# SSD output transposed one projection later, first convolutions ahead of the dt chain, and gates dealt anew, in a hybrid encoder layer

## Chip, cores and metric

One core of a Trainium2 chip runs the whole layer in one program. The metric is the device time of that program in microseconds (us), the median of several runs. Engines: PE (TensorE, matmuls), DVE (VectorE), ACT (ScalarE), POOL (GpSimd), SP (SyncE, which only issues transfers here).

## What is computed

A sequence of 1024 tokens of width 1024 goes through one encoder layer, in fp32. The reference, cut to what matters here:

```python
h = rmsnorm(x, norm_mix)
proj = h @ w_in            # q, k, v | z | x, B, C | dt | gate_a, gate_b
attn = windowed_gqa_sink(q, k, v, attn_sink)       # 16 heads, 4 kv heads, |t-s| <= 128
ssd = ssd_branch(z, xbc, dt_raw, ...)              # 8 groups of 4 heads
merged = sigmoid(gate_a) * (attn @ w_attn_branch) + sigmoid(gate_b) * (ssd @ w_ssd_branch)
x = x + merged @ w_out
x = x + cross_attention(rmsnorm(x, norm_cross), rmsnorm(mem, norm_mem), w_xq, w_xkv, w_xo)
x = x + square(relu(rmsnorm(x, norm_ffn) @ w_up)) @ w_down
return rmsnorm(x, norm_final)

def ssd_branch(z, xbc, dt_raw, ...):
    xs, B, C = split(silu(depthwise_conv_5(xbc) + conv_b))
    dt = softplus(dt_raw + dt_bias)                # 32 heads, two directions
    y = scan_forward(xs, dt, B, C) + scan_backward(xs, dt, B, C) + d_skip * xs
    y = grouped_rmsnorm(y * silu(z)) * norm_g
```

Both scans go in 8 chunks of 128 tokens: within a chunk y is (C B^T times a decay matrix) times x, and between chunks a state is carried on.

## The kernel before

Every fp32 matmul is made of three matmuls on a high and a low part of its operands (`mm3`, L78 to L86): one of 128x512 outputs per k, 8 k's and two halves make one projection of 128 channels by 1024 tokens, 48 matmuls, which land in one PSUM tile of two banks (pool pg, two buffers). Smaller PSUM tiles (pool pp, four buffers of one bank) hold the states, steps and transposes. Weights come as raw tiles of 128x1024 through SP's queue; ACT makes the high part (`whi`, L66), POOL the low part (`wlo`, L67).

Start: after the norm, `dt_part` (L210 to L290) projects dt and works out softplus, running sums (two scans, L270 and L271) and exponentials on DVE and ACT, the dt chain; its results are transposed on PE (`dtt`, L289).

SSD phase: for each of 8 groups a list of jobs (L535 to L571) gives PE's order by hand: four convolution projections (`conv_job`: two x tiles, B, C), one gate projection (`gate_job`), and z (`z_job`). A job yields after each chunk of three matmuls, and a table hangs other work on the chunk's number: while group g is projected, group g-1 is scanned. `conv_post` (L340 to L358) takes a convolution from PSUM: one ACT operation (L345) and four taps on DVE (L349, L351) that read PSUM and so hold its tile, then tanh on ACT (L353) and a closing DVE operation (L354). `state` (L443) makes chunk states, `back` (L460) runs the backward recursion on POOL, `prep` (L467) makes the decay matrix ef of the next chunk: two loads of rows on ACT's queue, two selects on POOL, eight exponentials on ACT (L484, L485), a sum (L486) and a product (L487) on DVE. `step` (L489) calls `prep` for the chunk below and does one chunk: matmuls with ef (L499) and with the state (yo, L503), then t from yo (L507, which frees the PSUM tile of yo), the D skip on POOL (L511, L513), sums and gate (L515 to L517), squares (L518), and after every fourth chunk the norm's scale on four yz tiles (L522). `yt` (L525) transposes four yz tiles into two PSUM tiles (L530), which ACT takes (`yts`, L532, one buffer) and SP writes to memory.

Only PE's order is fixed by hand in this phase; the Tile scheduler orders the other engines' queues.

Attention (`attn_phase`, L574) goes over 4 kv heads and 8 blocks of queries: scores (sps, L657), softmax, transposes (pt, L680), values (op, L689 and L690). Its blocks are woven with gate projections (`gate_block`, L705), which the table `ATT_GATES` assigns to kv heads, and with the next kv head's projections. The merge (`merge_cross_phase`, L709) begins with the gates of `END_GATES` (L727); beside them it loads the attention's and the SSD's outputs (at, yk: SP's queue, then a copy on ACT, L723, and a difference on DVE, L724), 8 and 16 tiles of 256 KB and three weights, into a pool that opens when the attention's pool is released. Its matmuls (mps) read those tiles in order, three for each of 24 tiles.

Of the kernel before, what the change touches and what calls it, by code (L numbers as in the profile page):

```python
# [29 lines left out]
ATT_GATES = ((11,), (12,), (13,), ())  # L30
# [67 lines left out]
def wsplit(w, nk=NK):  # L98
    hi = w[0].rearrange("p (k c) -> p k c", k=nk)
    lo = w[1].rearrange("p (k c) -> p k c", k=nk)  # L100
    return [(hi[:, k], lo[:, k]) for k in range(nk)]
# [108 lines left out]
def dt_part(kx, ins, dr, p0):  # L210
# [99 lines left out]

def ssd_phase(kx, ins, dr):
# [4 lines left out]
    with tc.tile_pool(name="p1", bufs=1) as sp, tc.manual_schedule(engines={mybir.EngineType.PE}):  # L316
# [7 lines left out]
        class Group:  # L324
            pass

        gs = []
        for g in range(NG):
            q = Group()
            q.g, q.hs, q.cx = g, slice(4 * g, 4 * g + 4), []  # L330
            gs.append(q)

        def fm_chunks(ps, w, halves=(0, 1)):
            ws = wsplit(w)
            for h in halves:
                for k in range(NK):
                    mm3(kx, ps[:, h * 512:(h + 1) * 512], ws[k], act_pair(kx.hT[h], k), k == 0, k == NK - 1)
                    yield

        def conv_post(q, i, ps):  # L340
            tag = ("cx", "cx", "cB", "cC")[i]
            j = 4 * q.g + i
            cw = lambda k: kx.cw[:, 5 * j + k:5 * j + k + 1]
            acc = ca.tile([P, S], F32, tag=tag, bufs=2 if i < 2 else 1, name=tag)
            A.activation(acc, ps, AF.Identity, bias=kx.cb[:, j:j + 1], scale=cw(2))  # L345
            for k in (1, 3, 0, 4):
                o = k - 2
                if o < 0:
                    V.scalar_tensor_tensor(acc[:, -o:], ps[:, :S + o], cw(k), acc[:, -o:], ALU.mult, ALU.add)  # L349
                else:  # L350
                    V.scalar_tensor_tensor(acc[:, :S - o], ps[:, o:], cw(k), acc[:, :S - o], ALU.mult, ALU.add)  # L351
            th = ca.tile([P, S], F32, tag="tab", bufs=2, name="th")
            A.activation(th, acc, AF.Tanh)  # L353
            V.scalar_tensor_tensor(acc, th, 1.0, acc, ALU.add, ALU.mult)  # L354
            if i < 2:
                q.cx.append(acc)
            else:
                setattr(q, ("BT", "CT")[i - 2], acc)  # L358

        def psum_g(name):  # L360
            return kx.pg.tile([P, S], F32, tag="g", name=name)

        def conv_job(q, i):
            def load():
                return wload(kx, ins["wssd"][q.g, i])

            def run(w):
                ps = psum_g("cps")
                yield from fm_chunks(ps, w)
                conv_post(q, i, ps)  # L370
            return load, run

        def first_job(q):
            def load():
                return [wload(kx, ins["wssd"][q.g, i]) for i in range(2)]

            def run(ws):
                pss = [psum_g("cps") for _ in range(2)]
                for h in range(2):
                    for i in range(2):  # L380
                        yield from fm_chunks(pss[i], ws[i], (h,))
                for i in range(2):
                    conv_post(q, i, pss[i])
            return load, run

        def gate_job(m):
            def load():
                return wload(kx, ins["wg"][m])

            def run(w):  # L390
                ps = psum_g("gps")
                yield from fm_chunks(ps, w)
                gt = ca.tile([P, 2, 512], F32, tag="tab", bufs=2, name="gt")
                for h in range(2):
                    A.activation(gt[:, h], ps[:, h * 512:(h + 1) * 512], AF.Tanh, scale=0.5)
                    nc.sync.dma_start(dr.gt[m][h], gt[:, h])
            return load, run
# [69 lines left out]
        def prep(q, c):  # L467
# [12 lines left out]
            q.ef = ef = sp.tile([P, 4, P], F32, tag="ef", bufs=3, name="ef")  # L480
# [8 lines left out]
        def step(q, c):  # L489
# [24 lines left out]
            y = q.yz[j] = sp.tile([P, 256], F32, tag="yz", bufs=6, name="yz")  # L514
# [25 lines left out]
        for g in range(NG):  # L540
            q, o = gs[g], gs[g - 1]
            scan = lambda *cs: [(step, o, c) for c in cs] if g else []
            if g == 0:
                job(first_job(q), {})
                job(gate_job(0), {})
                job(conv_job(q, 2), {})
                job(conv_job(q, 3), {8: [(tm_x, q)]})
            else:
                job(conv_job(q, 0), {8: [(step, o, 7)], 16: [(step, o, 6)]})
                job(conv_job(q, 1), {8: [(step, o, 5)], 16: [(step, o, 4)]})  # L550
                job(gate_job(g), {8: [(step, o, 3)], 16: [(step, o, 2), (yt, o)]})
                job(conv_job(q, 2), {8: [(step, o, 1)], 16: [(step, o, 0)]})
# [6 lines left out]
        job(gate_job(8), {5: [(step, q, 7)], 10: [(step, q, 6)], 16: [(step, q, 5)]})  # L559
        job(gate_job(9), {5: [(step, q, 4)], 10: [(step, q, 3)], 16: [(step, q, 2), (yt, q)]})  # L560
        job(gate_job(10), {5: [(step, q, 1)], 10: [(step, q, 0)]})
# [519 lines left out]
```

## Time and profile before

| what | value |
|---|---|
| median of 3 runs | 2541.56 us (2540.14 to 2542.85) |
| the profiled execution | 2542.49 us |
| its span, first to last instruction | 2540.7 us |
| mean granted clock of PE | 0.986 |
| busy: PE, PE's weight loads | 96%, 80% |
| busy: DVE, ACT, POOL | 49%, 40%, 37% |
| moved by DMA | 212 MB, 84 GB/s |

The times in views of the trace count from the first instruction of the profiled execution. The granted clock is a share of full speed (2.4 GHz); its other level is half of it (1.2 GHz), so that a stretch with a value between the two had some of both. A wait is idle time of an engine that ended when another one released it. Busy times are averages over stages with different limits; what an edit is worth is read at its place.

### The profile page before, as it was taken

What the parts mean: (1) busy time and instruction counts of PE and PEld (TensorE: products, weight loads), DVE (VectorE), ACT (ScalarE), POOL (GpSimd) and SP (SyncE); (2) the same over time, 40 slices, a digit from 0 to 9 for tenths busy, and PEclk for the clock granted to TensorE, in tenths of its full rate; (3) what the DMA queues carried; (4) which work ended last, traced back from release to release, by engine and by line L of the source; (5) the groups of instructions that cost most, each with busy time, mean ns of one, the idle gap of its engine ahead of it and who ended that gap; (6) DMA issues with size and microseconds to landing.
All of it is one profiled execution on the core that took longest, in us unless ns stands there. A gap on an engine that the chain in (4) does not pass through costs nothing.

```text
span 2540.7 us, 32190 instructions
## 1 busy us (share of the span) xinstructions
PE 2446.7 (96%) x12348; PEld 2035.1 (80%) x12348; DVE 1241.4 (49%) x2033; ACT 1024.6 (40%) x2114; POOL 934.5 (37%) x808
## 2 busy tenths in 40 slices
PE   7899999999999999999989999999999999999998
PEld 6687887878778788877768878888988888888887
DVE  5656555565655553465554252335543434343435
ACT  5436445463644544576664242235432121212112
POOL 4334526354452643354444444224332131312120
PEclk9899999999999999999999999999999999999999
DMA  6313223132322312111115363411121010101101
GB/s 221 100 50 117 67 84 111 56 116 64 103 75 76 116 66 76 48 40 55 51 37 204 133 224 128 171 50 67 59 75 67 34 67 34 66 35 58 42 34 67
DMA packets 135913, 212.20 MB, mean 84 GB/s; under 512 B 9680, under 2 KB 84560, under 8 KB 135760
## 3 DMA queue, kind: packets, MB, share of 16 engines
q1 hardware_dynamic: 65152, 171.86, 19.6%
q10 hardware_dynamic: 70608, 38.28, 5.3%
q8 instruction: 97, 1.59, 0.3%
q14 instruction: 56, 0.46, 0.1%
HBM read 183.63 MB, written 26.48 MB: 83 GB/s over the span
## 4 chain that ended last, share of the span: by engine, by line
PE 74%; POOL 7%; DVE 6%; ACT 5%; DMA 4%; issue 3%; POOLq 0%; SPq 0%; ACTq 0%; DVEq 0%
PE ups L81 5%; PE ups L86 5%; PE ups L85 5%; PE dps L86 4%; PE dps L81 4%; PE dps L85 4%; PE mps L85 3%; PE mps L86 3%; PE mps L81 3%; DMA rows<-d_cs 3%; PE zp L86 2%; PE zp L85 2%; PE zp L81 2%; PE cps L81 2%; PE cps L85 2%
## 5 line engine op out<-in xcount | busy, mean ns | idle before, releaser
L67 POOL TENSOR_TENSOR wlo<-raw,whi 128x1024 fp32r<-128x1024 f32 x170 | 412.4, 2427 | 458.8 <-ACT whi L66 441.7
L66 ACT ACTIVATE whi<-raw 128x1024 fp32r<-128x1024 f32 x172 | 181.6, 1056 | 356.8 <-PE mps L85 117.4
L962 DVE TENSOR_TENSOR x<-x,dps 128x512 f32<-128x512 f32 x256 | 175.8, 688 | 124.6 <-PE dps L86 123.0
L67 POOL TENSOR_TENSOR wdl<-raw,wdh 128x1024 fp32r<-128x1024 f32 x32 | 76.0, 2396 | 423.2 <-ACT wdh L66 423.2
L81 PE MATMUL cps<-kt,whi 128*128 128x512 f32 x512 | 217.0, 424 | 0.0
L86 PE MATMUL cps<-kt,wlo 128*128 128x512 f32 x512 | 202.6, 396 | 0.0
L85 PE MATMUL cps<-kt,whi 128*128 128x512 f32 x512 | 202.5, 395 | 0.0
L81 PE MATMUL ups<-kt,whi 128*128 128x512 f32 x512 | 199.7, 390 | 0.0
L85 PE MATMUL ups<-kt,whi 128*128 128x512 f32 x512 | 199.4, 390 | 0.0
L86 PE MATMUL ups<-kt,wlo 128*128 128x512 f32 x512 | 199.2, 389 | 0.0
L81 PE MATMUL dps<-wdh,u 128*128 128x512 f32 x512 | 199.2, 389 | 0.0
L85 PE MATMUL dps<-wdl,u 128*128 128x512 f32 x512 | 199.2, 389 | 0.0
L86 PE MATMUL dps<-wdh,u 128*128 128x512 f32 x512 | 199.2, 389 | 0.0
L936 DVE TENSOR_TENSOR u<-ups,ru 128x512 f32<-128x512 f32 x64 | 44.2, 690 | 256.4 <-ACT ru L934 254.6
L66 ACT ACTIVATE wdh<-raw 128x1024 fp32r<-128x1024 f32 x32 | 32.3, 1053 | 229.9 <-PE dps L86 229.7
L81 PE MATMUL gps<-kt,whi 128*128 128x512 f32 x256 | 109.7, 429 | 12.6 <-DVE cx L351 12.6
L85 PEld LDWEIGHTS cps<-kt,whi 128*128 128x128 f32 x512 | 98.6, 193 | 24.2 <-issue 5.0
L81 PEld LDWEIGHTS cps<-kt,whi 128*128 128x128 f32 x512 | 98.6, 193 | 24.0 <-issue 5.0
L86 PEld LDWEIGHTS cps<-kt,wlo 128*128 128x128 f32 x512 | 98.1, 192 | 21.7
L464 POOL TENSOR_TENSOR cb_t<-prev,dec 128x256 f32<-128x256 f32 x48 | 32.2, 672 | 224.8 <-ACT prev L458 222.2
L81 PEld LDWEIGHTS ups<-kt,whi 128*128 128x128 f32 x512 | 96.1, 188 | 20.4 <-ACT kt L143 0.3
L85 PEld LDWEIGHTS ups<-kt,whi 128*128 128x128 f32 x512 | 96.1, 188 | 20.0 <-DVE kt L144 0.2
(312 smaller groups left out, 6482.8 us busy)
## 6 DMA issues: line engine op xcount, KB each, us to landing
rows<-d_cs ACTq DMA_DIRECT2D x128, 256.0 KB, 4.2
raw<-in_wssd_dram SPq DMA_DIRECT2D x48, 512.0 KB, 3.8
raw<-in_wsb_dram SPq DMA_DIRECT2D x32, 512.0 KB, 3.2
raw<-in_wup_dram SPq DMA_DIRECT2D x32, 512.0 KB, 3.2
raw<-in_wdn_dram SPq DMA_DIRECT2D x32, 512.0 KB, 3.2
x<-in_x_dram SPq DMA_DIRECT2D x16, 512.0 KB, 7.2
raw<-in_wg_dram SPq DMA_DIRECT2D x16, 512.0 KB, 4.2
d_y<-yts SPq DMA_DIRECT2D x32, 256.0 KB, 2.8
```

The lines of the kernel that those rows point to most:

```text
L66: nc.scalar.activation(hi, raw, AF.Copy)
L67: (eng or nc.gpsimd).tensor_tensor(lo, raw, hi.bitcast(F32), ALU.subtract)
L81: i = mm(out, l[0], r[0], start=first, stop=False)
L85: mm(out, l[0], r[1], start=False, stop=False)
L86: mm(out, l[1], r[0], start=False, stop=last)
L464: G.tensor_tensor(heads(t), heads(prev[:, c, 1]), decay(q, 1, c), ALU.mult)
L936: V.tensor_tensor(u2, pv, r, ALU.mult)
L962: V.tensor_tensor(xh, xh, ps, ALU.add)
```

## The change

Four edits, of order and buffers alone:

- The first `yt` of a group moves from chunk 16 of the gate job, right behind step 2, to chunk 16 of the next convolution job, ahead of step 0. For this yz has 8 buffers instead of 6, and ef 2 instead of 3.
- The first two convolutions of group 0 are issued in `dt_part`, ahead of the dt chain (`first_tiles`); group 0's gate moves behind the convolutions of B and C.
- The last group's steps hang on the gates 8 and 9 alone, every four chunks, instead of on 8, 9 and 10.
- Gates 10 to 13 are dealt to the four kv heads; the last kv head had none. Gates 14 and 15 stay in the merge's code.

```diff
-ATT_GATES = ((11,), (12,), (13,), ())
+ATT_GATES = ((10,), (11,), (12,), (13,))
 END_GATES = (14, 15)
...
             A.activation(e[o:o + 32], ps[64 + 32 * d:96 + 32 * d, h * N:(h + 1) * N], AF.Copy)
+    first_tiles(kx, ins)
     V.tensor_tensor(u, u, e, ALU.add)
...
+def first_tiles(kx, ins):
+
+    q = kx.first = Group(0)
+    ws = [wload(kx, ins["wssd"][0, i]) for i in range(2)]
+    pss = [psum_g(kx, "cps") for _ in range(2)]
+    for h in range(2):
+        for i in range(2):
+            for _ in fm_chunks(kx, pss[i], ws[i], (h,)):
+                pass
+    for i in range(2):
+        conv_post(kx, q, i, pss[i])
...
-            q.ef = ef = sp.tile([P, 4, P], F32, tag="ef", bufs=3, name="ef")
+            q.ef = ef = sp.tile([P, 4, P], F32, tag="ef", bufs=2, name="ef")
...
-            y = q.yz[j] = sp.tile([P, 256], F32, tag="yz", bufs=6, name="yz")
+            y = q.yz[j] = sp.tile([P, 256], F32, tag="yz", bufs=8, name="yz")
...
             if g == 0:
-                job(first_job(q), {})
-                job(gate_job(0), {})
                 job(conv_job(q, 2), {})
-                job(conv_job(q, 3), {8: [(tm_x, q)]})
+                job(conv_job(q, 3), {})
+                job(gate_job(0), {8: [(tm_x, q)]})
             else:
                 job(conv_job(q, 0), {8: [(step, o, 7)], 16: [(step, o, 6)]})
                 job(conv_job(q, 1), {8: [(step, o, 5)], 16: [(step, o, 4)]})
-                job(gate_job(g), {8: [(step, o, 3)], 16: [(step, o, 2), (yt, o)]})
-                job(conv_job(q, 2), {8: [(step, o, 1)], 16: [(step, o, 0)]})
+                job(gate_job(g), {8: [(step, o, 3)], 16: [(step, o, 2)]})
+                job(conv_job(q, 2), {8: [(step, o, 1)], 16: [(yt, o), (step, o, 0)]})
                 job(conv_job(q, 3), {8: [(tm_x, q)], 16: [(yt, o)]})
...
         q = gs[7]
-        job(gate_job(8), {5: [(step, q, 7)], 10: [(step, q, 6)], 16: [(step, q, 5)]})
-        job(gate_job(9), {5: [(step, q, 4)], 10: [(step, q, 3)], 16: [(step, q, 2), (yt, q)]})
-        job(gate_job(10), {5: [(step, q, 1)], 10: [(step, q, 0)]})
+        job(gate_job(8), {4: [(step, q, 7)], 8: [(step, q, 6)], 12: [(step, q, 5)], 16: [(step, q, 4)]})
+        job(gate_job(9), {4: [(step, q, 3)], 8: [(step, q, 2)], 12: [(step, q, 1)], 16: [(yt, q), (step, q, 0)]})
```

The first job of before did in `ssd_phase` what `first_tiles` does in `dt_part`, and `Group`, `fm_chunks`, `psum_g` and `conv_post` move out of `ssd_phase` with their text unchanged but for the argument kx. Lines shift by a few; L503, L507 and L534 of the changed kernel are L499, L503 and L530 of before.

How the queues change, at three places. First PE at the first yt of a group (group 0's scan; yz_1743, 1680, 1601 and 1538 are the four yz tiles of steps 7 to 4, yo_1887 that of step 2, yo_1962 that of step 1; yt_1907 in the one and yt_2006 in the other is the second yt tile). Before:

```order
L479 MATMUL cb_1869<-cC_1146,cB_1051 128x128
L499 MATMUL cb_1805<-xtok_1097,ef_1807 128x64 x4
L503 MATMUL yo_1887<-prev_1182,cC_1146 128x512
L530 MATMUL yt_1899<-ident_128,yz_1743 128x128
L530 MATMUL yt_1899<-ident_128,yz_1680 128x128
L530 MATMUL yt_1899<-ident_128,yz_1601 128x128
L530 MATMUL yt_1899<-ident_128,yz_1538 128x128
L530 MATMUL yt_1907<-ident_128,yz_1743 128x128
L530 MATMUL yt_1907<-ident_128,yz_1680 128x128
L530 MATMUL yt_1907<-ident_128,yz_1601 128x128
L530 MATMUL yt_1907<-ident_128,yz_1538 128x128
L81 MATMUL cps_1926<-kt_223,whi_1765 128x512
```

Now:

```order
L86 MATMUL cps_1910<-kt_442,wlo_1766 128x512
L534 MATMUL yt_1998<-ident_128,yz_1743 128x128
L534 MATMUL yt_1998<-ident_128,yz_1680 128x128
L534 MATMUL yt_1998<-ident_128,yz_1601 128x128
L534 MATMUL yt_1998<-ident_128,yz_1538 128x128
L534 MATMUL yt_2006<-ident_128,yz_1743 128x128
L534 MATMUL yt_2006<-ident_128,yz_1680 128x128
L534 MATMUL yt_2006<-ident_128,yz_1601 128x128
L534 MATMUL yt_2006<-ident_128,yz_1538 128x128
L503 MATMUL cb_1944<-xtok_1101,ef_1946 128x64 x4
L507 MATMUL yo_2018<-prev_1182,cC_1055 128x256
L81 MATMUL cps_2058<-kt_223,whi_1904 128x512
```

The eight transposes stood right behind step 2's yo; now they come behind step 1 and 24 matmuls of the next convolution, and step 0 (cb_1944, yo_2018) comes behind them. In PSUM yt_1907 has the slot of yo_1887, issued five rows ahead of it, and yt_2006 that of yo_1962, issued 24 matmuls ahead of the first row shown.

Second DVE at the start (cx_918 and cx_927 before, cx_840 and cx_849 now, are the first two convolutions, with four taps each; cs the running sums; the rest is the dt chain). Before:

```order
L267 MEMSET r_756 64x4
L268 MEMSET r_756 64x4
L260 COPY_PREDICATED acc_721<-mk_750,e_718 128x512
L349 SCALAR_TENSOR_TENSOR cx_918<-cps_820,cols_176,cx_918 128x1023
L262 SCALAR_TENSOR_TENSOR acc_721<-u_717,acc_721 128x512
L351 SCALAR_TENSOR_TENSOR cx_918<-cps_820,cols_176,cx_918 128x1023
L263 TENSOR_SCALAR u_717<-e_718,ea_677 128x512
L349 SCALAR_TENSOR_TENSOR cx_918<-cps_820,cols_176,cx_918 128x1022
L270 SCALAR_TENSOR_TENSOR cs_760<-r_756,u_717 64x512
L271 SCALAR_TENSOR_TENSOR cs_760<-r_756,u_717 64x512
L275 COPY end_764<-cs_760 64x4
L351 SCALAR_TENSOR_TENSOR cx_918<-cps_820,cols_176,cx_918 128x1022
```

Now:

```order
L257 TENSOR_TENSOR e_718<-e_718,acc_721 128x512
L340 SCALAR_TENSOR_TENSOR cx_840<-cps_742,cols_176,cx_840 128x1023
L258 SCALAR_TENSOR_TENSOR e_718<-u_717,e_718 128x512
L342 SCALAR_TENSOR_TENSOR cx_840<-cps_742,cols_176,cx_840 128x1023
L261 COPY_PREDICATED acc_721<-mk_878,e_718 128x512
L340 SCALAR_TENSOR_TENSOR cx_840<-cps_742,cols_176,cx_840 128x1022
L267 MEMSET r_884 128x512
L342 SCALAR_TENSOR_TENSOR cx_840<-cps_742,cols_176,cx_840 128x1022
L340 SCALAR_TENSOR_TENSOR cx_849<-cps_743,cols_176,cx_849 128x1023
L263 SCALAR_TENSOR_TENSOR acc_721<-u_717,acc_721 128x512
L342 SCALAR_TENSOR_TENSOR cx_849<-cps_743,cols_176,cx_849 128x1023
L345 SCALAR_TENSOR_TENSOR cx_840<-th_846,cx_840 128x1024
```

The taps of both convolutions have moved up; between the first convolution's four taps stand three operations of the chain (one a memset) instead of five, and the chain's scans, which stood ahead of the second convolution, come behind its taps. On PE 47 matmuls of the third convolution stand between the point that waits for the first convolution's tile and the dt transposes; before, 11 of gate 0 did.

Third PE in the last kv head, where scores of a block begin. Before:

```order
L657 MATMUL sps_11962<-kh_10869,q_11690 128x384
L658 MATMUL sps_11962<-kl_10870,q_11690 128x384
L657 MATMUL sps_11966<-kh_10869,q_11693 128x384
L658 MATMUL sps_11966<-kl_10870,q_11693 128x384
L657 MATMUL sps_11970<-kh_10869,q_11751 128x384
L658 MATMUL sps_11970<-kl_10870,q_11751 128x384
L657 MATMUL sps_11974<-kh_10869,q_11754 128x384
L658 MATMUL sps_11974<-kl_10870,q_11754 128x384
L680 MATMUL pt_11991<-ident_128,t4_11823 128x128 x4
```

Now:

```order
L659 MATMUL sps_11902<-kh_10809,q_11630 128x384
L660 MATMUL sps_11902<-kl_10810,q_11630 128x384
L659 MATMUL sps_11906<-kh_10809,q_11633 128x384
L660 MATMUL sps_11906<-kl_10810,q_11633 128x384
L81 MATMUL gps_12265<-kt_442,whi_12259 128x512
L85 MATMUL gps_12265<-kt_442,whi_12259 128x512
L659 MATMUL sps_11910<-kh_10809,q_11691 128x384
L660 MATMUL sps_11910<-kl_10810,q_11691 128x384
L86 MATMUL gps_12265<-kt_442,wlo_12260 128x512
L659 MATMUL sps_11914<-kh_10809,q_11694 128x384
L660 MATMUL sps_11914<-kl_10810,q_11694 128x384
L81 MATMUL gps_12265<-kt_442,whi_12259 128x512
```

A gate's matmuls (gps_12265, gate 13) stand between the scores, as they do in the first three kv heads in both kernels; before, the last kv head had none, and gates 14 and 15 followed as two blocks of 48. Now gate 14 is woven in as well, with the first four matmuls of gate 15, and 44 of gate 15 follow the last op.

## Rows read from the trace of the kernel before

**Rows 1.** The page, part 1: busy time of each engine, share of the span, instructions

```profile
PE 2446.7 (96%) x12348; PEld 2035.1 (80%) x12348; DVE 1241.4 (49%) x2033; ACT 1024.6 (40%) x2114; POOL 934.5 (37%) x808
```

**Rows 2.** Waits of PE: line, releaser: us in total, times, longest

```profile
PE yt L530 <- DVE t L507: 27.9, 8, 3.7
PE gps L81 <- DVE cx L351: 12.6, 1, 12.6
...
PE op L689 <- ACT ph L683: 5.9, 5, 3.1
PE tm L426 <- DVE cB L354: 4.7, 4, 2.1
```

**Rows 3.** Stretches: start:end, length, engines' busy us (instructions), PEclk, DMA share, GB/s

```profile
1163.00:1223.00 60.00, 59.33 (x290) 47.04 (x290) 34.76 (x93) 38.54 (x87) 24.85 (x30) 1.00 0.12 38
1264.00:1324.00 60.00, 46.31 (x201) 34.34 (x202) 35.24 (x116) 41.48 (x111) 27.18 (x41) 0.86 0.09 25
```

**Rows 4.** Stretches that begin where a wait of PE ends, columns as above

```profile
94.20:98.20 4.00, 3.96 (x10) 3.17 (x11) 3.97 (x6) 2.93 (x4) 0.00 (x0) 0.55 0.04 6
211.00:215.00 4.00, 4.00 (x14) 3.40 (x15) 0.91 (x3) 2.37 (x7) 3.46 (x4) 0.65 0.66 217
...
430.30:436.30 6.00, 6.00 (x18) 4.91 (x19) 2.24 (x4) 3.02 (x10) 5.29 (x5) 0.55 0.80 247
539.90:543.90 4.00, 4.00 (x20) 3.38 (x21) 0.87 (x3) 2.39 (x7) 3.46 (x4) 1.00 0.70 216
...
651.80:657.80 6.00, 6.00 (x17) 4.90 (x18) 2.26 (x4) 3.01 (x10) 5.31 (x5) 0.52 0.78 243
761.60:767.60 6.00, 6.00 (x18) 4.90 (x19) 2.27 (x4) 3.01 (x10) 5.32 (x5) 0.57 0.71 246
...
968.40:972.40 4.00, 4.00 (x13) 3.37 (x14) 0.96 (x3) 1.75 (x4) 3.19 (x3) 0.60 0.64 211
```

**Rows 5.** Timeline around two yt tiles: start, us, engine, line, operation [idle before, releaser]

```profile
207.89 1.23 DVE L354 SCALAR_TENSOR_TENSOR cx<-th,cx 128x1024 f32<-128x1024 f32 x1 [0.53 <-ACT th L353]
...
210.23 0.68 DVE L507 TENSOR_TENSOR t<-yo,ecs 128x512 f32<-128x512 f32 x1
...
210.97 1.12 PE L530 MATMUL yt<-ident,yz 128*128 128x128 f32 x4 [3.68 <-DVE t L507]
...
968.36 1.11 PE L530 MATMUL yt<-ident,yz 128*128 128x128 f32 x4 [3.10 <-DVE t L507]
```

**Rows 6.** Timeline, first convolution, columns as above

```profile
82.17 0.69 DVE L256 TENSOR_TENSOR e<-e,acc 128x512 f32<-128x512 f32 x1
...
84.72 1.27 DVE L349 SCALAR_TENSOR_TENSOR cx<-cps,cols,cx 128x1023 f32<-128x1023 f32 x1
...
91.50 1.22 DVE L271 TENSOR_TENSOR_SCAN cs<-r,u 64x512 f32<-64x512 f32 x1
...
94.24 0.77 PE L81 MATMUL gps<-kt,whi 128*128 128x512 f32 x1 [12.62 <-DVE cx L351]
```

**Rows 7.** Timeline, end of the SSD phase, columns as above

```profile
942.81 0.95 DVE L516 TENSOR_TENSOR yz<-yz,p 128x256 f32<-128x256 f32 x1 [4.91 <-POOL p L511]
...
944.96 1.27 ACT L484 ACTIVATE ef<-rows,ebias 128x128 f32<-128x128 f32 x4
...
945.64 1.00 PE L499 MATMUL cb<-xtok,ef 128*128 128x64 f32 x8
```

**Rows 8.** Stretch in the merge's loads, columns as of the stretches above

```profile
1330.00:1340.00 10.00, 10.00 (x46) 8.29 (x45) 4.91 (x8) 6.41 (x11) 0.00 (x0) 1.00 0.92 308
```

**Rows 9.** Timeline, merge's loads, columns as of the timelines above

```profile
1331.17 1.22 ACT L723 ACTIVATE at<-at 128x512 fp32r<-128x512 f32 x2 [7.73 <-DMA at<-d_at]
...
1343.83 0.40 PE L81 MATMUL mps<-at,whi 128*128 128x512 f32 x1
1344.06 0.40 PE L85 MATMUL mps<-at,whi 128*128 128x512 f32 x1
...
1350.72 3.76 DVE L724 TENSOR_TENSOR yk<-yk 128x512 fp32r<-128x512 f32 x5 [1.46 <-ACT yk L723]
```

More of the change, by code (lines that the diff above doesn't have):

```diff
@@ L308, in pin_next_matmul, with __init__, fm_chunks, psum_g @@
     kx.pin = True
+class Group:
+    def __init__(self, g):
+        self.g, self.hs, self.cx = g, slice(4 * g, 4 * g + 4), []
+def fm_chunks(kx, ps, w, halves=(0, 1)):
+    ws = wsplit(w)
+    for h in halves:
+        for k in range(NK):
+            mm3(kx, ps[:, h * 512:(h + 1) * 512], ws[k], act_pair(kx.hT[h], k), k == 0, k == NK - 1)
+            yield
+def psum_g(kx, name):
+    return kx.pg.tile([P, S], F32, tag="g", name=name)
+def conv_post(kx, q, i, ps):
+    V, A = kx.nc.vector, kx.nc.scalar
+    ca = kx.conv_pool
+    tag = ("cx", "cx", "cB", "cC")[i]
+    j = 4 * q.g + i
+    cw = lambda k: kx.cw[:, 5 * j + k:5 * j + k + 1]
+    acc = ca.tile([P, S], F32, tag=tag, bufs=2 if i < 2 else 1, name=tag)
+    A.activation(acc, ps, AF.Identity, bias=kx.cb[:, j:j + 1], scale=cw(2))
+    for k in (1, 3, 0, 4):
+        o = k - 2
+        if o < 0:
+            V.scalar_tensor_tensor(acc[:, -o:], ps[:, :S + o], cw(k), acc[:, -o:], ALU.mult, ALU.add)
+        else:
+            V.scalar_tensor_tensor(acc[:, :S - o], ps[:, o:], cw(k), acc[:, :S - o], ALU.mult, ALU.add)
+    th = ca.tile([P, S], F32, tag="tab", bufs=2, name="th")
+    A.activation(th, acc, AF.Tanh)
+    V.scalar_tensor_tensor(acc, th, 1.0, acc, ALU.add, ALU.mult)
+    if i < 2:
+        q.cx.append(acc)
+    else:
+        setattr(q, ("BT", "CT")[i - 2], acc)
+def first_tiles(kx, ins):
[8 more added lines that the diff above has]
+        conv_post(kx, q, i, pss[i])
 def ssd_phase(kx, ins, dr):
@@ L322, in heads @@
             return ap.rearrange("p (h q) -> p h q", h=4)
[L324 to L361, printed above, removed]
+        gs = [kx.first] + [Group(g) for g in range(1, NG)]
         def conv_job(q, i):
@@ L367, in run @@
             def run(w):
[L368 to L383, printed above, removed]
+                ps = psum_g(kx, "cps")
+                yield from fm_chunks(kx, ps, w)
+                conv_post(kx, q, i, ps)
             return load, run
@@ L390, in run @@
             def run(w):
-                ps = psum_g("gps")
-                yield from fm_chunks(ps, w)
+                ps = psum_g(kx, "gps")
+                yield from fm_chunks(kx, ps, w)
                 gt = ca.tile([P, 2, 512], F32, tag="tab", bufs=2, name="gt")
```

## Prediction, made before the changed kernel had run

> **What bounds the kernel now.** First the page's busy times: PE is busy for 2446.7 of 2540.7 us and no other engine for half of that [rows 1]. So 94 us is all that waiting costs, and a change that leaves PE's work alone can win only from these 94 us and from matmuls that ran at the lower clock. Second, PE's waits: the largest is that of the yt transposes for DVE's t, 27.9 us in eight waits; then one wait of 12.6 us for the first convolution; then many small ones of the attention [rows 2]. Third, busy time and granted clock in stretches: the 60 us of the last attention pass (kv 3) have PE busy 46.3 us at clock 0.86, where 60 us of the pass before have 59.3 us at 1.00 [rows 3]; after five of the seven yt waits inside the groups the clock is at 0.52 to 0.65, after the other two, of which one is shown, at 1.00 [rows 4]. Last, timelines of the places that the change touches, and one stretch of the merge [rows 5 to 9]: what ended the wait there, and what stood ahead of it on the releasing engine. The chip's own noise on this kernel is about 0.2%, 5 us; the profiled execution took 2542.5, 0.9 above the median.
>
> **1. yt a projection later.** The second of the two yt tiles takes the PSUM slot of step 2's yo, and PE reaches it right behind that step. The slot is free when DVE has made t (L507), and t stands behind a convolution's last operation (L354, 1.23 us, itself late for a tanh) and the products of ef: t ends at 210.91, PE goes on at 210.97 after 3.68 us [rows 5]. By the new order 24 matmuls of the convolution stand between step 1 and yt, and the slot is step 1's. At 0.23 us a matmul [rows 9] that is 5.5 us, more than the longest wait of 3.7 [rows 2]; and the projection that ends just ahead of it is a gate, which leaves DVE no convolution to finish. So I cost the wait at nothing: 27.9 less the tail's 3.10 [rows 2, 5] is 24.8 us gained. If that cover fails, t is late by what is left of 3.7.
> The clock after those waits: a stretch of length L at clock g has lost L(1-g). Two stretches of 4 us at 0.65 (the second, at 320 us, reads the same), and 6 us each at 0.55, 0.52 and 0.57 [rows 4]: 1.4 + 1.4 + 2.7 + 2.9 + 2.6 = 11.0 us.
> What can be late next is step 0, which now stands behind yt, and ef: with two buffers instead of three the exponentials of one step need the matmuls of the step two before to be done. Such a set is 1.27 us for four activations [rows 7], twice per step, and two DVE operations of 0.68 like L507 [rows 5], together 3.9 us. I take 3 us for new small waits in the 64 steps (bounds 0, and 64 sets of 1.27 us as a rival below), and 2 us off the tm waits of 4.7 [rows 2], which now follow a queue that did not stall (bounds 0 and 4.7). **Part 1: -24.8 - 11.0 + 3 - 2 = -34.8 (-42 to -20).** The eight yz buffers hold four blocks three steps longer and cost nothing else.
>
> **2. First two convolutions ahead of the dt chain.** PE waits 12.62 us because the first convolution's PSUM tile is free only after four taps, which start at 84.72 and end at 94.1, as operations of the dt chain stand between them [rows 6]. In the new DVE order (the second below the change) the first tap follows the operation that ended at 82.17 + 0.69 = 82.86 [rows 6], and three chain operations stand between the taps: 4 taps of 1.27 and these, 1.7 us by what stood between 82.86 and 84.72, end at 89.6. PE starts 4.5 us earlier. But the chain, whose last scan began at 91.50 [rows 6], now ends behind the second convolution's four taps and one closing operation, 5 x 1.27 = 6.4 us later. Before, 11 matmuls stood between the wait and the dt transposes, 10 of them in 4 us at clock 0.55 [rows 4], so these began at 98.6 and did not wait; now they can begin at 105.0 at the latest, where PE, after 47 matmuls of 0.23 and the same 1.8 us lost to the clock [rows 4], is at 102.2. It waits 2.8 us. **Part 2: -4.5 + 2.8 = -1.7, say -2 (-4.5 if the chain is ready in time, +2 if DVE's order adds more).**
>
> **3. End of the SSD phase.** Gate 10 leaves, and eight steps stand in two gates, 12 matmuls apart. Step 5 comes after 12 chunks of three matmuls instead of 16: 12 x 0.23 = 2.8 us earlier. Its ef was only just in time: DVE waited 4.91 us for POOL, whose backward loop ended late (942.81), and PE's step began at 945.64 [rows 7]. POOL does not get faster, so nearly all the 2.8 us comes back as a wait, 2.6. For the steps behind it I take 2 us together, each step's two sets of exponentials being 2.5 us against 2.8 us of matmuls between steps, and for the last yt, now behind step 0 alone, 1 us. Gained is the yt wait of 3.1 [rows 5] and 4 x (1 - 0.60) = 1.6 of clock [rows 4]. **Part 3: 2.6 + 2 + 1 - 4.7 = +1 (-4.7 to +6).**
>
> **4. Attention and merge.** In kv 0 to 2 a gate's matmuls and the next projections are woven into the blocks; kv 3 had none, hence 13.7 us of idle time in 60 against 0.7 [rows 3], op's wait for ph among it [rows 2]. Now gates 13 and 14 are woven into kv 3 as they were into the earlier passes (the third order). I take kv 3 to become like the pass before: 13.0 us of idle time and 46.3 x 0.14 = 6.5 us of clock go.
> Price: behind the last op stood 96 matmuls of gates 14 and 15, 22.1 us that covered the loads of the merge. Now 44 are left, 10.1 us. The loads can't start sooner, since their tiles reuse the attention's space. Before, the last op ended at 1343.83 - 22.1 = 1321.7, the first at tile reached ACT at 1331.17, and the last yk tile was done at 1350.72 + 3.76 = 1354.5, which is 32.8 us behind the last op [rows 9]. PE now wants that tile after 10.1 us and 23 x 3 matmuls, 15.9 us: at 26.0. The difference, 6.8 us, is the upper bound; gate ends that stood between ACT's copies come sooner now, so I take 5, and 0 as the lower bound. It comes in small pieces, tile by tile.
> 24 tiles of 256 KB and three weights of 512 KB are 7.9 MB; at the 308 GB/s of that stretch [rows 8] they take 25.5 us, so the transfer sets the time and not the queue of copies. The Trainium skill, DMA: Bandwidth & Descriptors, Bandwidth, has about 358 GB/s as the limit from memory to the core; by that the loads would end 3.5 us sooner and the stall be an estimated 1.5. The row here lies 14% under it and decides.
> **Part 4: -13.0 - 6.5 + 5 = -14.5 (-20 to -6).** Gate 10 only changes places with gate 11, and so on: their matmuls are PE work wherever they stand.
>
> **Sum:** -34.8 - 2 + 1 - 14.5 = -50.3, from 2542.5 to 2492.2 for a profiled execution, 0.9 less for the median: **2491 us**. Own range 2473 to 2507, the parts' errors being partly of opposite sign.
>
> **Rivals.**
> *The clock stays low.* The waits shrink to fractions of a microsecond, but there are enough of them around the steps and in kv 3 for the clock to go on falling. For it: the stretch at 968, where steps are dense, is at 0.60 after a wait no longer than those at 540 [rows 4, 5]. Against it: the pass before has 0.7 us of idle time in small pieces at 1.00 [rows 3], and the stretch at 540 is at 1.00 behind a yt wait. Then 11.0 + 6.5 = 17.5 us don't come: 2508. The Trainium skill, TensorE: Matmul & The Clock Gate, on a second failure mode through cycling PSUM tiles, tells of just this, micro-idles between groups of matmuls that keep the clock swinging; the pass with small gaps at 1.00 disagrees so far.
> *The slot's wait only moves.* The change does not do what it says: yt still waits as long for a yo slot, since t may again stand behind work that DVE took first. For it: DVE's order is the scheduler's, and at 207.89 it put a convolution's end ahead of t [rows 5]. Against it: 5.5 us of matmuls now lie between. Then 24.8 + 11.0 = 35.8 stay: 2527.
> *Slower: two ef buffers bind every step.* Place: the exponentials (L484 before). Each set can start only when PE has done the step two before, so if ACT's queue puts weight copies and closing activations ahead of it, PE waits at the step's own matmuls. If each of 64 steps waits one set of 1.27 us, 81 us are lost and 50 gained: 2573. It decides from 50.3/64 = 0.79 us a step. For it: PE's step at 945.64 followed its ef at once [rows 7]. Against it: in a group two steps are two times 24 matmuls, 11 us, apart without their own work, for a path of 3.9 us.
>
> **How the numbers follow.** Forecast 0.62, clock 0.14, moved wait 0.12, ef 0.07; 0.05 for the start and the loads both at their bad ends, some 10 us above the forecast. The range takes the forecast's own range, the clock rival and these last: 2472 to 2512, 0.81. Faster by over 0.2%: all but the ef case and a little of the moved wait with other losses, 0.91; within 0.2%: 0.03; slower: 0.06.
>
> **What would show it.** Right: yt gone from PE's waits or under 3 us; clock 1.00 in all seven places behind yt; 1264 to 1324's counterpart busy above 57 of 60 at 1.00; the first wait near 8 us, with a second of some 3 us at the dt transposes; small waits of mps for at and yk, 3 to 7 us in all; a wait of some 2.6 us at the third step of gate 8. Wrong: PE's waits name ef at the steps for over 10 us; yt still waits for t; kv 3 busy but below 0.95; or the start loses more at the transposes than it gains.

## The result and the profile after

The changed kernel took 2506.49 us (median of 4 runs, 2505.01 to 2507.81), the kernel before 2542.2 us on the same chip: ratio 0.9856, 95% interval 0.9839 to 0.9873. That is 36 us faster, where 50 were forecast; the time lies in the stated range, just inside the upper end of the forecast's own (2507). None of the four edits was run alone against the kernel before; what each gave is read from its place in the trace.

The page's first lines and its busy times, against [rows 1]:

```profile
span 2504.2 us, 32169 instructions
...
PE 2434.0 (97%) x12348; PEld 2023.8 (81%) x12348; DVE 1284.3 (51%) x2033; ACT 1025.3 (41%) x2114; POOL 935.5 (37%) x808
```
The span fell by 36.5 us: PE's time without work from 94.0 to 70.2 us (23.8), and its busy time by 12.7 us, which is put down to the clock, since the matmuls are the same. PE's waits (line, releaser: us in total, times, longest), against [rows 2]:

```profile
PE cb L503 <- DVE ef L491: 14.6, 10, 2.3
...
PE cps L81 <- DVE cx L342: 8.8, 1, 8.8
PE tm L430 <- ACT yts L536: 5.8, 5, 1.6
PE mps L85 <- DVE yk L726: 3.4, 2, 2.0
PE yt L534 <- DVE t L511: 2.7, 1, 2.7
PE mps L81 <- ACT at L725: 2.2, 2, 1.5
...
PE yt L534 <- ACT yz L526: 1.2, 1, 1.2
PE dtt L290 <- DVE r L284: 0.9, 1, 0.9
```
The 27.9 us of yt for t are down to one wait of 2.7, and op for ph and tm for cB are gone from the top. In their place stands a name that was not there: the step's own matmuls wait for ef, 14.6 us in ten waits. Stretches (start:end, length, busy us of PE, PEld, DVE, ACT, POOL, PEclk, DMA share, GB/s), the first behind the start's wait, four behind waits for ef at step 2, one behind the tail's yt, then the last kv head and the merge's loads, against [rows 3, 4, 8]:

```profile
90.60:94.60 4.00, 3.99 (x10) 3.13 (x11) 4.00 (x5) 2.28 (x2) 0.00 (x0) 0.50 0.00 0
203.90:207.90 4.00, 4.00 (x20) 3.13 (x21) 3.11 (x7) 3.65 (x11) 1.45 (x3) 1.00 0.43 121
417.60:423.60 6.00, 6.00 (x22) 4.46 (x23) 4.31 (x8) 5.48 (x14) 2.62 (x5) 0.72 0.54 176
524.70:528.70 4.00, 4.00 (x20) 3.13 (x21) 3.17 (x7) 3.61 (x11) 1.50 (x3) 1.00 0.39 112
...
844.70:850.70 6.00, 6.00 (x22) 4.31 (x23) 4.30 (x9) 5.48 (x14) 2.62 (x5) 0.72 0.53 171
948.20:952.20 4.00, 4.00 (x16) 3.72 (x17) 1.54 (x4) 2.36 (x6) 0.69 (x1) 0.50 0.13 52
1231.40:1291.40 60.00, 58.65 (x298) 45.19 (x297) 38.66 (x116) 45.63 (x118) 31.08 (x42) 1.00 0.16 48
1300.00:1320.00 20.00, 15.66 (x56) 11.58 (x57) 16.00 (x23) 16.83 (x28) 4.73 (x2) 0.92 0.97 341
```
Behind five of the seven waits for ef at step 2 the clock stays at 1.00, three of them not shown; behind two it falls to 0.72 over 6 us. The last kv head is now busy for 58.65 of 60 us at 1.00, where it had 46.31 at 0.86.

Where the time came from shows when PE's work is cut at matmuls that both kernels have:

| stretch of PE | before, us | after, us | difference | forecast |
|---|---|---|---|---|
| start, to the first zp matmul (131.94, 129.45) | 131.9 | 129.4 | -2.5 | -2 |
| groups, to the end of the last zp (930.42, 906.43) | 798.5 | 777.0 | -21.5 | -34.8 |
| end of SSD and attention, to the first mps (1343.83, 1300.30) | 413.4 | 393.9 | -19.5 | +1 - 19.5 |
| merge's mps, to the end of the last (1610.31, 1573.71) | 266.5 | 273.4 | +6.9 | +5 |
| the rest, to PE's last matmul | 922.4 | 922.5 | 0 | 0 |

Gate 10 lies in the third stretch in both kernels. So the start, the attention and the merge came out within 2 us of the forecast, and 13.3 of the 14 us that are missing are missing in the groups.

There PE's waits of 0.1 us or more fell from 32.0 us (yt for t 24.8, tm 7.1) to 18.0: 12.3 for ef and 5.8 of tm for yts. The other 7.6 us are left for the clock. The 12.3 us are nine waits, seven of them of 1.4 to 1.7 us, one a group, at step 2, which make 11.4. How the first of these comes about shows the timeline of DVE, POOL and PE in the first group:

```profile
196.62 2.42 POOL L67 TENSOR_TENSOR wlo<-raw,whi 128x1024 fp32r<-128x1024 f32 x1 [1.63 <-ACT whi L66]
...
197.54 1.78 DVE L521 TENSOR_TENSOR yz<-yz,zs 128x256 f32<-128x256 f32 x1
...
199.25 1.10 DVE L490 TENSOR_TENSOR ef<-ef,eb 128x512 f32<-128x512 f32 x1
...
200.87 1.64 DVE L345 SCALAR_TENSOR_TENSOR cx<-th,cx 128x1024 f32<-128x1024 f32 x1
...
202.42 0.68 DVE L118 TENSOR_SCALAR rv<-ss 128x4 f32<-128x4 f32 x1
203.02 0.67 DVE L491 TENSOR_TENSOR ef<-ef,cb 128x512 f32<-128x512 f32 x1
...
203.84 0.96 PE L503 MATMUL cb<-xtok,ef 128*128 128x64 f32 x7 [1.43 <-DVE ef L491]
203.95 0.67 DVE L490 TENSOR_TENSOR ef<-ef,eb 128x512 f32<-128x512 f32 x1
```
L521 takes 1.78 us instead of 0.42 beside a weight split on POOL; the convolution's closing operation (L345) and the norm's (L118) stand ahead of the product of ef (L491); PE gets it at 203.84, 1.43 us late. The sum of ef (L490) too takes longer ahead of the wait, 1.10 us, than behind it, 0.67. The start's two waits:

```profile
90.61 0.77 PE L81 MATMUL cps<-kt,whi 128*128 128x512 f32 x1 [8.76 <-DVE cx L342]
...
104.29 0.66 PE L290 MATMUL dtt<-ident,r 128*128 128x128 f32 x4 [0.87 <-DVE r L284]
```

### The profile page after: what moved, and what is told of

The parts are those of the page before. It is cut to its first block, busy times and chain, and to the rows that moved or that the text cites. A ratio compares the mean times of both kernels' runs of the same rounds, so it can differ in the third digit from the quotient of the medians.

```text
span 2504.2 us, 32169 instructions
## 1 busy us (share of the span) xinstructions
PE 2434.0 (97%) x12348; PEld 2023.8 (81%) x12348; DVE 1284.3 (51%) x2033; ACT 1025.3 (41%) x2114; POOL 935.5 (37%) x808
## 4 chain that ended last, share of the span: by engine, by line
PE 68%; DVE 12%; POOL 7%; ACT 6%; issue 4%; DMA 2%; SPq 0%; POOLq 0%; ACTq 0%; DVEq 0%
PE ups L81 5%; PE ups L86 5%; PE ups L85 5%; PE dps L86 4%; PE dps L85 4%; PE dps L81 4%; PE mps L85 3%; PE mps L86 3%; PE mps L81 3%; PE zp L86 2%; PE zp L85 2%; PE zp L81 2%; PE st L454 2%; POOL wlo L67 2%; DVE cx L342 2%
## 5 line engine op out<-in xcount | busy, mean ns | idle before, releaser
L81 PEld LDWEIGHTS cps<-kt,whi 128*128 128x128 f32 x512 | 97.5, 190 | 34.8 <-issue 16.1
L81 PEld LDWEIGHTS dps<-wdh,u 128*128 128x128 f32 x512 | 96.1, 188 | 19.9
```

Of the source, the lines that this page charges most:

```text
L81: i = mm(out, l[0], r[0], start=first, stop=False)
```

## Experiments

Each run was timed in three rounds against the kernel before on its chip, whose medians were 2544.2, 2541.8, 2542.3 and 2542.9 us in the four sessions; times below are medians, with the ratio's interval. Sums of waits in the groups (from the first zp to the last, waits of 0.1 us or more) are worked out from the traces.

**Three ef buffers.** Room for it comes from xs.

```diff
-            xs = sp.tile([P, 2, 4, 64], F32, tag="xs", bufs=2, name="xs")
+            xs = sp.tile([P, 2, 4, 64], F32, tag="xs", bufs=1, name="xs")
...
-            q.ef = ef = sp.tile([P, 4, P], F32, tag="ef", bufs=2, name="ef")
+            q.ef = ef = sp.tile([P, 4, P], F32, tag="ef", bufs=3, name="ef")
```

> The changed kernel with three ef buffers again (the room comes from xs, one buffer instead of two). Theory A, two ef buffers make PE wait at step 2 of every group (seven waits of 1.4 to 1.7 us, 11.5 us, for ef): they vanish, and the time falls from 2506 to about 2495. Theory B, DVE is behind with its queue there (a convolution's closing operation and the norm's stand ahead of the product of ef): the seven waits stay at 1.4 to 1.7 us and the time at 2504 to 2509. If xs with one buffer costs anything it shows as waits of st.

Measured: 2506.72 us (2500.35 to 2510.57), ratio 0.9853 (0.9834 to 0.9872). PE's waits from 120 to 945 us:

```profile
PE tm L430 <- ACT yts L536: 12.6, 8, 1.8
PE yt L534 <- ACT xtok L431: 5.1, 8, 0.8
PE cb L503 <- DVE ef L491: 2.2, 1, 2.2
PE st L454 <- DVE xs L450: 1.4, 1, 1.4
```
The seven waits for ef are gone; the one that is left stands in the last group's steps, behind the groups. So theory A is right that the wait hangs on the number of buffers; the runs with two yts buffers below, which differ in ef's buffers alone, say the same (12.1 us of waits in the groups against none). It is wrong about the time, and B, right about the time, is wrong about the wait. By what way the buffer makes the wait this run does not tell, since three things change with it. ACT's exponentials of ef wait less often for PE to give a buffer back (all of the run, us and times; the changed kernel, then this run):

```profile
  PE cb L503: 50.4, 16
```
```profile
  PE cb L503: 40.3, 8
```
DVE's order is another, and its lengthened operations, told in the last section, cost 14 us instead of 43. PE's waits in the groups add up to 19.5 us instead of 18.0: what ef gave back, tm for yts (12.6 for 5.8) and yt for xtok took.

**Steps 3, 2 and 1 later.**

```diff
-                job(gate_job(g), {8: [(step, o, 3)], 16: [(step, o, 2)]})
-                job(conv_job(q, 2), {8: [(step, o, 1)], 16: [(yt, o), (step, o, 0)]})
+                job(gate_job(g), {11: [(step, o, 3)]})
+                job(conv_job(q, 2), {2: [(step, o, 2)], 9: [(step, o, 1)], 16: [(yt, o), (step, o, 0)]})
```

> The changed kernel with step 3 three chunks later (chunk 11 of the gate), step 2 two chunks later (chunk 2 of the next convolution) and step 1 one chunk later (chunk 9). DVE gets 1.4 us more until step 2 and 2.0 us more until step 3. Theory B: the seven waits for ef of 1.4 to 1.7 us fall to 0.3 or less each, and the time to about 2495, a few us less if the clock falls after them go too. Theory A expects shorter waits as well, since only step 2 moves and not the step it depends on; so this run sizes the wait and does not tell the two apart. Against both: the yt transposes behind step 1 come to wait for t by up to 1 us each, as step 1 is nearer to them.

Measured: 2504.89 us (2501.98 to 2505.46), ratio 0.9846 (0.9831 to 0.9860). No wait for ef is left in the groups, as expected, but tm for yts is at 12.3 us and the sum at 14.8: 3.3 us less waiting and 1.6 us less time, where 11 were expected. In the traced execution, the fastest of its four, the groups are 5.4 us shorter than in that of the changed kernel.

**Two buffers for yts**, by sharing those of xs.

```diff
-                yo_s = sp.tile([P, 512], F32, tag="yts", bufs=1, name="yts")
+                yo_s = sp.tile([P, 512], F32, tag="xs", bufs=2, name="yts")
```

> The changed kernel with two buffers for the transposed output on its way to memory (yts takes those of xs, which the next z job uses), ef still two. Three ef buffers alone took the waits for ef away (12.3 us) and gave none of it back as time: the waits of tm for yts grew from 5.8 to 12.6 us. Theory C: ef and yts bind one behind the other, so each alone only hands the wait on. Then here the waits of tm for yts vanish (5.8 us) while those for ef stay at 11 to 13 us: 2500 to 2502. Rival: the late thing is ACT's queue, not the buffer: tm still waits 4 us or more and the time stays at 2505 to 2508.

Measured: 2517.72 us (2513.02 to 2522.65), ratio 0.9913 (0.9889 to 0.9937), slower than the changed kernel.

```profile
PE cb L503 <- DVE ef L491: 14.4, 8, 2.3
PE st L454 <- DVE xs L450: 6.1, 7, 0.9
PE tm L430 <- ACT yts L536: 4.4, 6, 1.3
```
tm still waits 4.4 us for ACT, and the shared buffers cost a wait of their own (st for xs, 6.1 us), so the time is a bound and no clean measure; but with the buffer added most of tm's wait is still there, as the rival said.

**Both: two for yts, three for ef.**

> The changed kernel with two buffers for yts (shared with xs) and three for ef. Theory C: with both, neither the waits for ef nor those of tm for yts are left; of the 18 us of waits in the groups over 13 go, and the falls of the clock behind them: 2485 to 2493, which is where the forecast put the changed kernel. Rival, DVE or ACT is behind with its queue: a third wait takes their place (yt for xtok, tm for cB, st for xs) and the time stays above 2500.

Measured: 2508.2 us (2504.9 to 2509.61), ratio 0.9871 (0.9848 to 0.9894).

```profile
PE tm L430 <- ACT yts L536: 14.1, 7, 2.0
PE st L454 <- DVE xs L450: 2.6, 3, 0.9
PE cb L503 <- DVE ef L491: 2.2, 1, 2.2
```
Theory C falls: with both buffers tm waits longer than ever, 14.1 us, and the sum in the groups is 18.8. ACT's own timeline at the first of these places says why:

```profile
235.44 0.69 ACT L489 ACTIVATE eb<-rows,ebias 128x128 f32<-128x128 f32 x2 [1.30 <-POOL rows L480]
236.04 1.04 ACT L66 ACTIVATE whi<-raw 128x1024 fp32r<-128x1024 f32 x1
236.99 1.24 ACT L536 ACTIVATE yts<-yt,cols 128x512 f32<-128x512 f32 x2
```
The two evacuations of yt stand behind exponentials that waited 1.30 us for POOL's select on the rows, and behind a weight copy of 1.04 us. Here it is ACT's queue that is late, not a buffer.

**yt at chunk 13**, with three ef buffers and one of xs.

```diff
-                job(conv_job(q, 3), {8: [(tm_x, q)], 16: [(yt, o)]})
+                job(conv_job(q, 3), {8: [(tm_x, q)], 13: [(yt, o)]})
```

> Three ef buffers and one of xs, as in the first experiment, and the second yt of a group at chunk 13 instead of 16 of the fourth convolution, 9 matmuls or 2.0 us earlier. With three ef buffers, with or without a second yts buffer, tm waited 12.6 to 14.1 us for the evacuation of the second yt tile, which stands on ACT behind exponentials and a weight copy. Theory E: that place on ACT's queue is what binds then, so a yt issued 2 us earlier takes 1 to 1.5 us off each of the 8 waits: tm for yts under 5 us, 2494 to 2499. Rival: yt itself comes to wait, for the norm's scale on yz, by as much as tm gains: 2503 to 2508.

Measured: 2512.15 us (2508.86 to 2517.91), ratio 0.9887 (0.9867 to 0.9906).

```profile
PE yt L534 <- ACT xtok L431: 19.4, 14, 2.7
```
tm for yts is gone, and yt has come to wait by more, not for the norm's scale but for ACT to take xtok out of PSUM: a miss on both sides, though the rival had the direction.

**One DVE addition less per step**, ef with two buffers.

```diff
                 G.tensor_tensor(p1, p1, t[:, 1], ALU.add)
+            G.tensor_tensor(p1, p1, t[:, d0], ALU.add)
...
-            V.tensor_tensor(y, cb[:, 256:], t[:, d0], ALU.add)
-            V.tensor_tensor(y, y, p1, ALU.add)
+            V.tensor_tensor(y, cb[:, 256:], p1, ALU.add)
```

> The changed kernel (two ef buffers) with one DVE addition per step less: the sum with p reads PSUM (cb plus p), and POOL adds t to p ahead of it. In the changed kernel 38 of 112 DVE operations on yz, whose operands all lie in SBUF, take 0.8 to 2.4 us instead of 0.42, 43 us in all, most of them beside a weight split on POOL; before, 7 did. Theory D: these meetings make DVE late for ef at step 2, and not the two buffers as such. Then DVE's long yz operations fall below 15 us, the waits for ef from 12.3 to under 4 us; what is gained as time may again go to tm for yts. Theory A (two buffers): the waits for ef stay at 10 us or more, although DVE has less to do.

Measured: 2567.12 us (2562.88 to 2567.34), ratio 1.0091 (1.0076 to 1.0106), slower than the kernel before.

```profile
PE cb L503 <- DVE ef L491: 20.6, 11, 3.2
PE yo L507 <- DVE yz L520: 17.5, 7, 4.2
```
Of DVE's operations on yz with both operands in SBUF the edit leaves 56 of 112; 29 of these take over 0.8 us, costing 23 us instead of 43, and PE waits longer for ef than before the edit. Theory D had expected under 15 us for them. But the edit also made DVE's sum, and with it the PSUM slot of cb, wait for POOL, 17.5 us of it seen by PE. So D is not shown, and not refuted either: the edit changed more than it was to test.

**Gate 14 kept behind the last op**, gate 13 issued ahead of the values of the last two blocks.

```diff
+                if kv == 3 and qb == 6:
+                    gate_block(kx, ins, dr, 13)
                 values(qb, t4s[qb])
-            for m in ATT_GATES[kv]:
+            for m in ATT_GATES[kv][:1 if kv < 3 else 0]:
```

> The changed kernel with gate 13 issued ahead of the last block of the last kv head, so that gates 14 and 15 both stay behind the last op, as in the kernel before, and only gate 13 is woven in. If gate 14 was missing as cover of the merge's loads, the waits of mps in the first tile (4.7 us) go, and the merge's matmuls from first to last take 266.5 us again instead of 273.4: 7 us gained. Price: the last kv head has 48 matmuls, 10.9 us, to fill 13.7 us of idle time, so 3 to 4 us of waits come back: 2502 to 2503. Rival: without gate 14 the last blocks are as bare as before (waits of 0.8 to 3 us for ph, with falls of the clock): 7 us or more come back, 2506 to 2510.

Measured: 2513.72 us (2513.12 to 2514.45), ratio 0.9883 (0.9868 to 0.9898). PE's waits from 1030 to 1340 us, and the stretch of the last kv head:

```profile
PE op L691 <- ACT ph L685: 3.8, 5, 2.3
PE sps L659 <- DVE nm L661: 1.7, 3, 0.8
```
```profile
1234.00:1294.00 60.00, 52.58 (x244) 39.17 (x243) 39.09 (x118) 44.01 (x116) 30.94 (x41) 0.91 0.14 41
```
The merge's matmuls take 266.5 us again, as forecast, so gate 14 was the cover that was missing. But gate 13 is used up in the first half of the last kv head, whose 60 us then have PE busy for 52.58 at clock 0.91: the rival. From the first kps matmul to the last op PE takes 340.5 us, where the changed kernel takes 338.4 with 52 matmuls, 11.8 us, more: so gate 14 in the last kv head is worth some 12 to 14 us (2 of the 14 are a longer wait of the tail's yt, ahead of that head), and costs 7 in the merge. The difference is near the 7 us that this run is slower.

**Gates dealt 10, none, 11, 12 with 13.**

```diff
-ATT_GATES = ((10,), (11,), (12,), (13,))
+ATT_GATES = ((10,), (), (11,), (12, 13))
```

> The changed kernel with the gates dealt 10, none, 11, and 12 with 13 to the four kv heads: the second kv head has the keys' projection of the next pair to weave in and gets no gate, the last gets two, and gates 14 (all but 4 matmuls) and 15 stay behind the last op. If gate 14 was missing as cover, the 4.7 us of waits in the merge's first tile and the other 2 us of its matmuls go, while the last kv head stays as full as in the changed kernel: 2499 to 2500. Rival: the second kv head is bare without a gate and loses 5 us or more to waits for ph and q: 2504 or above.

Measured: 2500.61 us (2497.74 to 2502.65), ratio 0.9844 (0.9825 to 0.9864): 5.9 us under the changed kernel, near the 6 to 7 expected. The last kv head's 60 us:

```profile
1221.00:1281.00 60.00, 58.67 (x298) 45.24 (x297) 38.65 (x116) 45.64 (x118) 31.08 (x42) 1.00 0.16 50
```
No wait for at or yk is left in the first mps tile; one of 4.7 us for a weight split on POOL stands in a later one, and the mps matmuls take 270.8 us.

**Gate 0 beside the first convolution.**

```diff
-    ws = [wload(kx, ins["wssd"][0, i]) for i in range(2)]
-    pss = [psum_g(kx, "cps") for _ in range(2)]
+    ws = [wload(kx, ins["wg"][0]), wload(kx, ins["wssd"][0, 0])]
+    pss = [psum_g(kx, n) for n in ("gps", "cps")]
...
+                job(conv_job(q, 1), {})
                 job(conv_job(q, 2), {})
-                job(conv_job(q, 3), {})
-                job(gate_job(0), {8: [(tm_x, q)]})
+                job(conv_job(q, 3), {8: [(tm_x, q)]})
```

> The changed kernel with gate 0 and the first convolution as the two tiles ahead of the dt chain, then the second, third and fourth convolution. A gate's PSUM tile is freed by two ACT operations of some 0.5 us and not by four taps on DVE. Theory: the 8.8 us wait was for that tile alone, so it goes, with 2 us of half clock behind it, and nothing new is late, the third convolution's tile having 48 matmuls, 10.9 us, more time: 2495 to 2497. Rival: the chain on DVE is the real bound and the wait only moves, to the dt transposes or to the next convolution's tile: 2503 to 2507.

Measured: 2503.76 us (2499.48 to 2507.01), ratio 0.9848 (0.9831 to 0.9864). In the trace the first zp matmul begins at 123.4 instead of 129.4 us: 6.0 us at this place. The wait is 4.1 us instead of 8.8, for the first convolution's tile still, a job later:

```profile
PE cps L81 <- DVE cx L342: 4.1, 1, 4.1
```
The median fell by only 2.7 us, and its runs spread over 7.5; the traced execution, the fastest, is 6.6 us under that of the changed kernel. The gain at the place is shown, its full size in the median is not.

**Combinations.** Gate 0 first, two yts and three ef buffers, and gates dealt 10, none, 11, 12 with 13:

> All that the other runs suggest in one: gate 0 beside the first convolution at the start, yts with two buffers and ef with three, and the gates dealt 10, none, 11, and 12 with 13. If the parts add up (6 us at the start, 13 to 18 in the groups, 7 in the merge): 2475 to 2482. If theory C is wrong: 2490 to 2495.

Measured: 2489.36 us (2487.35 to 2493.86), ratio 0.9803 (0.9782 to 0.9824): the start and the gates add up, the groups gave nothing (18.0 us of waits). The same with one xs buffer instead of shared ones, and yt at chunk 13:

> The combination so far (gate 0 beside the first convolution; gates dealt 10, none, 11, 12 with 13) with three ef buffers, one of xs, and yt at chunk 13. The combination with two yts buffers took 2489 us, with 13.3 us of waits of tm for yts and 4.4 of st for xs. If theory E holds 8 to 12 us of these go: 2477 to 2482. If not, 2487 to 2491.

Measured: 2499.35 us (2495.45 to 2499.92), ratio 0.9825 (0.9811 to 0.9840): a miss, by the same wait of yt for xtok as above (20.4 us). The last run takes the better of the two and moves the transposes of B four chunks later and the chunk states, but for the last, two:

```diff
-            at = {8 * c + 8: [(state, q, c)] for c in range(NT)}
-            at[2] = [(tm_b, q)]
+            at = {8 * c + 10 if c < 7 else 64: [(state, q, c)] for c in range(NT)}
+            at[6] = [(tm_b, q)]
```

> The best combination (gate 0 first, two yts and three ef buffers, gates dealt 10, none, 11, 12 with 13; 2489 us) with the transposes of B (tm_b) at chunk 6 of the z job instead of 2, and the state operations but the last two chunks later. There PE waits 13.3 us in 7 places for ACT to take the second yt tile, whose PSUM slot tm needs; 4 chunks of three 128x256 matmuls are 1.4 us more for ACT. Theory F, four PSUM slots are handed round and PE meets whichever evacuation is late: the same waits would come back elsewhere (st for xs or btok) and the time stays at 2486 to 2492. Rival, that one wait is a matter of place: 1.2 to 1.4 us of each of the 7 go, tm for yts falls under 5 us, and the time to 2479 to 2483.

Measured: 2486.76 us (2481.86 to 2489.9), ratio 0.9780 (0.9757 to 0.9803). It is the fastest median of all, 20 us under the changed kernel, though no more than 2.6 under the first combination, and the two intervals overlap.

```profile
PE st L457 <- DVE xs L453: 11.2, 7, 1.6
PE tm L433 <- ACT yts L539: 5.5, 7, 1.5
```
tm for yts fell from 13.3 to 5.5 us and st for xs rose from 4.4 to 11.2; the sum is 16.9 for 18.0. As F had it, the wait moved; since the states moved as well, it is no clean test of the place of B's transposes.

## Why the prediction was right, and where it was short

**The slot's wait (part 1), right.** 24.8 us of yt for t in the groups are gone, all of it. The rival that it only moves to another yo slot fell; the clock rival fell too, though not wholly: of the 11.0 us lost behind yt, and 1.4 behind a wait of tm at 572 us, two falls of 6 x 0.28 = 1.7 us each are left.

**The step that failed** is "I take 3 us for new small waits in the 64 steps". They were 12.3 us for ef, where the forecast had bounds and a mechanism for them, and the rival of two ef buffers was priced as 64 equal waits or none. Nearly all of it is seven waits, one a group, at step 2, where DVE comes out of two convolutions with its queue full. With three buffers they are gone. The "2 us off the tm waits" was 1.4, the clock's 11.0 was 7.6 (9.0 by the falls just told; pieces under 0.1 us take 0.2 of the difference, the rest is open). -24.8 + 12.3 - 1.4 - 7.6 is the measured -21.5. One of the prediction's own signs of being wrong, PE's waits naming ef at the steps for over 10 us, came true. The time stayed in the range because the range was wide enough for it: the 13.3 us missing in the groups fill nearly all of the room between the forecast and its upper end.

**What the sizing overlooked** the runs show further on: the waits in the groups are not a sum of causes that can be taken away one at a time.

| kernel | ef | tm for yts | other | sum in the groups, us |
|---|---|---|---|---|
| changed | 12.3 | 5.8 | 0 | 18.0 |
| three ef buffers | 0 | 12.6 | 6.9 | 19.5 |
| steps later | 0 | 12.3 | 2.5 | 14.8 |
| two yts buffers | 12.1 | 4.4 | 6.1 | 22.7 |
| both | 0 | 14.1 | 4.7 | 18.8 |
| yt at chunk 13 | 0.2 | 0 | 22.6 | 22.8 |
| one addition less | 20.7 | 8.6 | 24.1 | 53.4 |
| the last run | 0.2 | 5.5 | 11.2 | 16.9 |

ef, yts, xtok and xs all come from ACT and DVE, which are free for a third of the groups' time or more (in the changed kernel DVE is busy for 63% of it, ACT for 49%), but whose queues, by the size of these waits, are some 2 us late between the second convolution and z; whichever product PE asks for there first would meet that delay. That these four share one cause is argued from the table and not shown; which operation one would have to take out of ACT's or DVE's queue is open, the one run that tried it (one addition less) having added a wait on POOL.

**The start (part 2), right in size, by other shares.** -2 forecast, -2.5 measured. The first wait is 8.76 us, 3.9 shorter (4.5 forecast); the second is 0.87 us instead of 2.8, and the clock behind the first lost 4 x 0.50 = 2.0.

**SSD's end and attention (parts 3 and 4), right, in part by errors that offset.** Together -19.5 for -18.5. The wait at gate 8's third step is 2.29 us (2.6 forecast). The tail's yt was costed at 1 us, and there are two waits, 2.67 for t and 1.21 for the norm's scale; behind the first the clock is at 0.50 (948.20 above), where the forecast had that fall gone. Against it, the 2 us for the steps behind the third did not come, and PE's other waits from the first kps matmul to the last op fell by 14.7 us, where 13.0 were forecast. The last kv head became as full as the others.

**The merge, right in the waits.** +6.9 us for 5, just over the upper bound of 6.8, which was for waits alone. Waits for at and yk are 4.7 us of it, and the clock in the 20 us of the loads is 0.92, which the forecast had left out: 1.6 us. Its loads ran at 341 GB/s, not at the 308 of before, nearer to the limit of about 358 that the Trainium skill names (DMA: Bandwidth & Descriptors, Bandwidth), and still the stall came, because the first at tile reached ACT 10 us behind the last op.

## What to carry to other kernels

A wait that is moved off a slot pays in full only if the engines that release it have time to spare: ask which product PE wants next from the same queue, and price that one at what the queue is behind, not at "small". Work that can stand anywhere (a gate) is worth most where nothing else fills and costs where it was the cover of loads; deal it by both, as the deal 10, none, 11, 12 with 13 does. When buffers are added and the sum of waits stays, as here, suspect the queue behind the buffers, and read its order next.

## Not expected of the hardware

DVE operations whose two operands both lie in SBUF took up to six times their length in the changed kernel. Three operations on 128x256 tiles, in the view of one line (count, shortest, median and longest ns, first and last start): L519 of the changed kernel, with one operand in PSUM, L521 of it, with both in SBUF, and L517 of before, which is the same operation as L521.

```profile
L519 DVE TENSOR_TENSOR yz<-cb,t x64: 410/416/426, 167.3 to 952.3; 128x256 f32<-128x256 f32 x64
```
```profile
L521 DVE TENSOR_TENSOR yz<-yz,zs x64: 407/427/2591, 172.4 to 953.2; 128x256 f32<-128x256 f32 x64
```
```profile
L517 DVE TENSOR_TENSOR yz<-yz,zs x64: 412/426/836, 175.2 to 982.1; 128x256 f32<-128x256 f32 x64
```
Of the 112 operations like L521 and L520 in the groups, 38 took over 0.8 us after the change, 43 us more than at 0.42 each, and 27 of those end within 0.6 us of the end of a weight split on POOL that ran when they began; before, 7 were as long, and none beside a split. The change moved them into each other's way without naming either, and it hangs on ef's buffers: with three of them 21 are long and 7 beside a split. The Trainium skill has contention of the two engines for SBUF when DVE has two SBUF inputs (GPSIMD Engine Reference, Specifications); the trace agrees, by L519, which reads PSUM and never takes over 426 ns. How much of the 12.3 us for ef comes from this no run settles. In all seven groups DVE has no gap in the last 7 us ahead of the late product of ef, and one operation on yz there, beside a split, takes 1.4 to 2.0 us more than 0.42; with the longer sum of ef (1.10 us for 0.67) that is 1.8 us or more, while PE waits 1.4 to 1.7. So in that order of DVE the lengthened operations alone are enough for the wait; that is worked out from durations, and not shown by a run. With three ef buffers the long operations cost 14 us instead of 43, and the time was the same.
